# A decoder trunk whose instruction order comes from a table of durations, with rotary scores on 128 rows

## The chip, the core and the metric

The kernel runs on one core of a Trainium2 chip. The metric is the device time of one execution in microseconds, as the median of repeated runs. On the core, TensorE (PE) does matmuls and transposes, VectorE (DVE) and ScalarE (ACT) do elementwise work, GpSimd (POOL) and SyncE (SP) issue DMAs here. PE has a weight load of its own before each matmul (PEld), which overlaps the matmul ahead.

## The reference

Two layers, each: half a SwiGLU step, a mixing block, half a SwiGLU step, on 256 tokens of 1024 features, all in float32:

```python
for l in range(2):
    h = h + 0.5 * swiglu(rms_norm(h, ln_ffn1[l]), ffn1_w13[l], ffn1_w2[l])      # 1024 -> 2 x 2816 -> 1024
    u = rms_norm(h, ln_mix[l])
    z, xbc, dt_raw, cq, ckv, kr, gates = split_cols(u @ w_in[l], IN_SPLIT_SIZES)
    y_ssd = ssd_branch(z, xbc, dt_raw, ...)     # conv of 4 taps, softplus(dt), chunked scan, 32 heads of 64, norm, w_out
    y_mla = mla_branch(cq, ckv, kr, cos, sin, ...)
    g = sigmoid(gates)
    h = h + (g[..., :1024] * y_ssd + g[..., 1024:] * y_mla) @ w_o[l]
    h = h + 0.5 * swiglu(rms_norm(h, ln_ffn2[l]), ffn2_w13[l], ffn2_w2[l])

# in mla_branch, for each of 8 heads: 128 unrotated and 64 rotated features
q = concatenate([q[..., :128], apply_rope(q[..., 128:], cos, sin)], -1)          # after rms_norm over 192
k = concatenate([k[..., :128], apply_rope(k[..., 128:], cos, sin)], -1)          # the rotated part is one for all heads
scores = where(causal, (q @ k.T) * 192 ** -0.5, -inf)                            # in two blocks of 128 queries
out = softmax(scores) @ v
```

## The kernel before

Activations lie transposed, features on the 128 partitions and the 256 tokens along the row. All weights come from HBM in float32 blocks, mostly 128x1024, in the order of use: SP's DMA brings a block to `st`, ACT rounds it to fp32r in `wh` (L152), DVE takes the difference `wl` (L153); four blocks are in flight. An activation operand (X, A, oT) is split the same way into a high and a low half. A product is then three matmuls of 256 columns per 128 features (`mm`, L169 to L171) or one of 512 and one of 256 (`mm2`, L178 and L179).

The stages of a layer are ffn 1, the mix and ffn 2. The mix begins with the projections for the latents of query and key-value, the softplus chain of dt (L501 to L524: a dozen small DVE steps, each of which reads the one before) and the cumulative sums of dA (L527, L528). Then follows a loop whose order `loop_order` writes out: for j in 0..7 the SSD of four heads (`ssd`), one attention head (`head`), and in between the convolution of the next channels, the projections of the next pair of heads, and so on. In the SSD the products of dec and xdt (L658) are 64 wide. A norm is: squares summed into acc, matmuls with ones (L241), a reciprocal root on DVE of nine small steps that each read the one before (`row_factor`, L249 and L216 to L224), and a broadcast by matmul (L256).

`head` works on head h, with i = h % 2 its place in a pair. It transposes the unrotated query and key (L761) and copies them to qkT; for i = 0 it also transposes the rotated query and key of the pair (L770: 64 features of each head, 128 rows together) and copies both to peT (L771). Scores are, for each of two blocks of queries, a product of qkT on 128 rows (L779) and one of peT on the 64 rows of head i (L780), added in PSUM, then a mask by matmul (L781). Softmax takes maxima on DVE (L784), exponentials with sums on ACT (L792), a reciprocal on DVE (L794) and a scaling on ACT; the result is transposed (L799) and multiplied with the values (L803, L804).

The program is written stage after stage. The scheduler of the framework (with its own timeline model, L905) decides the order on each engine, under the dependences of tiles and the numbers of buffers; in each ffn but the first, and in the mix, `issue_after` holds a part back until a named instruction (L388, L390, L437). An instruction waits on its own engine's queue, so what stands behind it waits too.

Of the kernel before, what the change touches and what calls it, by code (L numbers as in the profile page):

```python
# [2 lines left out]

# [1 line left out]

# [13 lines left out]
P = 128  # L19
L = 2  # L20
T = 256
# [14 lines left out]
XSB, ZB = 2, 1  # L36
STBUF = 4
GB, SB, HB = 4, 2, 2


V_LN1, V_LNM, V_LN2 = 0, 8, 16
# [16 lines left out]
NC_ = 672  # L58


class Build:
    def __init__(self, ctx, tc, a, out):
        self.tc, self.nc, self.a, self.out = tc, tc.nc, a, out
        nc = self.nc
        pool = lambda n, b=1, **k: ctx.enter_context(tc.tile_pool(name=n, bufs=b, **k))
# [142 lines left out]
    def rsqrt(self, x, n, tag):  # L208

        nc = self.nc  # L210
        y = self.tmp(tag + "y", [P, n])
        t = self.tmp(tag + "t", [P, n])
        tt, stt = nc.vector.tensor_tensor, nc.vector.scalar_tensor_tensor
        c = 0.703952253
        s = math.sqrt(0.375 * c)
        nc.vector.tensor_scalar(out=y.bitcast(I32), in0=x.bitcast(I32), scalar1=-0.5, scalar2=float(0x5F1FFFF9),  # L216
                                op0=ALU.mult, op1=ALU.add)
        tt(out=t, in0=y, in1=y, op=ALU.mult)
        stt(out=t, in0=t, scalar=-1.0, in1=x, op0=ALU.mult, op1=ALU.mult)
# [4 lines left out]
        self.last = stt(out=y, in0=t, scalar=5.0 * s * s, in1=y, op0=ALU.add, op1=ALU.mult).ins  # L224
        return y

    def square_into(self, acc, src, first):
# [8 lines left out]
    def row_ms(self, acc, scale, tag):  # L236

        nc = self.nc
        ps = self.sps()
        for c in range(2):  # L240
            self.summed = nc.tensor.matmul(ps[:, c:c + 1], lhsT=acc[:, c * P:(c + 1) * P], rhs=self.ones,  # L241
                                           start=True, stop=True).ins
        return ps

    def row_factor(self, acc, n, tag):
# [43 lines left out]
    def tables(self, cb, pos):  # L289
# [11 lines left out]
        for c in range(2):  # L301
            nc.vector.tensor_scalar(out=ang[:, c * 32:(c + 1) * 32], in0=inv, scalar1=posf[:, c:c + 1], scalar2=None,
                                    op0=ALU.mult)
        two_pi = 2.0 * math.pi
        parts, rest = [], two_pi
        for bits in (9, 9, 9):
# [70 lines left out]
    def ffn(self, l, which, X, Xn, gain_next, late=lambda: None):  # L377
# [5 lines left out]
        first = not self.used  # L383
        for i in range(KF):
            gu = self.tmp("t2", [P, 2, T])
            with ExitStack() as order:
# [4 lines left out]
                for g in range(2):  # L391
                    ps = self.gps()
                    m = KD // (2 if self.used < 4 else 1)
                    for k in range(0, KD, m):
                        self.mm2(ps, self.w("w13"), m, X, k, k == 0, k + m == KD)
                    self.halves(gu[:, g, :], ps)
# [21 lines left out]
    def mix(self, l, X0, Xn, gain, gain_next):  # L418
# [15 lines left out]
            self.square_into(acc2[q], ps, i in (0, 4))  # L434


        with self.tc.issue_after(self.last):  # L437
            ps = self.gps()[:, :T]
            self.mm(ps, self.w("dk"), KD, X0, 0, True, True)
            pg = self.gps()  # L440
            for g in range(2):
                self.mm(pg[:, g * T:(g + 1) * T], self.w("gate"), KD, X0, 0, g == 0, g == 1)
            latent(0)
# [59 lines left out]
        e = self.tmp("dte", [P, 2, 32], bufs=1)  # L503
        stt(out=e, in0=x, scalar=-1.0, in1=x, op0=ALU.mult, op1=ALU.max)
        act(out=e, in_=e, func=AF.Exp, scale=-1.0)
        d = self.tmp("dtd", [P, 2, 32], bufs=1)
# [4 lines left out]
        q = self.tmp("dtq", [P, 2, 32], bufs=1)  # L511
# [238 lines left out]
    def head(self, S, h):  # L750
# [11 lines left out]
        act(out=qkT[:, 0, :], in_=pn[:, :T], func=AF.Copy, scale=v[:, V_GQ:V_GQ + 1])  # L762
        act(out=qkT[:, 1, :], in_=pn[:, T:], func=AF.Copy, scale=v[:, V_GK:V_GK + 1])
        if i == 0:
            peT = self.tmp("peT", [P, 2, T], bufs=1)
# [41 lines left out]
    def run(self):  # L807
# [10 lines left out]
        for l in range(L):  # L818
# [91 lines left out]
```

## Time and profile before

| | us |
|---|---|
| median of 3 runs (lowest, highest) | 1468.09 (1467.69, 1468.92) |
| the profiled execution, its time and its span | 1469.72, 1467.8 |
| PE busy | 1451.8 |
| PE weight loads | 1304.8 |
| DVE busy | 1114.6 |
| ACT busy | 911.8 |

Busy time is the sum over the span. An engine's idle time costs something only where the chain of work that ends last goes through it. A matmul's end is modelled, so neighbouring ones overlap in the rows: the cost of one is read from its start to the start of the next. x2 in a timeline row means two equal instructions in succession; a float32 matmul shows as two passes.

### The profile page before, as it was taken

What the parts mean: (1) busy time and instruction counts of PE and PEld (TensorE: products, weight loads), DVE (VectorE), ACT (ScalarE), POOL (GpSimd) and SP (SyncE); (2) the same over time, 40 slices, a digit from 0 to 9 for tenths busy, and PEclk for the clock granted to TensorE, in tenths of its full rate; (3) what the DMA queues carried; (4) which work ended last, traced back from release to release, by engine and by line L of the source; (5) the groups of instructions that cost most, each with busy time, mean ns of one, the idle gap of its engine ahead of it and who ended that gap; (6) DMA issues with size and microseconds to landing.
All of it is one profiled execution on the core that took longest, in us unless ns stands there. A gap on an engine that the chain in (4) does not pass through costs nothing.

```text
span 1467.8 us, 25011 instructions
## 1 busy us (share of the span) xinstructions
PE 1451.8 (99%) x9418; PEld 1304.8 (89%) x9418; DVE 1114.6 (76%) x2080; ACT 911.8 (62%) x1738; POOL 18.5 (1%) x38
## 2 busy tenths in 40 slices
PE   7999999999999999999999999999999999999999
PEld 6888899899888999888888888997998889988888
DVE  7877679888877677777678776888888576688764
ACT  6555556988775456555455554678888654565542
POOL 0000000000000000000000000000000000000000
PEclk9999999999999999999999999999999999999999
DMA  7556655555444555556655566565554445555563
GB/s 254 184 186 178 192 176 182 183 160 157 152 144 158 188 179 188 191 189 183 193 191 191 188 180 195 178 192 155 166 169 139 154 165 190 175 190 193 187 197 109
DMA packets 75977, 261.43 MB, mean 178 GB/s; under 512 B 8880, under 2 KB 11184, under 8 KB 75856
## 3 DMA queue, kind: packets, MB, share of 16 engines
q1 hardware_dynamic: 73232, 251.37, 53.3%
q0 software_dynamic: 2624, 8.46, 1.9%
q8 instruction: 74, 1.21, 0.3%
q14 instruction: 47, 0.39, 0.1%
HBM read 258.68 MB, written 1.11 MB: 177 GB/s over the span
## 4 chain that ended last, share of the span: by engine, by line
PE 97%; DVE 1%; ACT 1%; issue 0%; DMA 0%; SPq 0%; DVEq 0%; ACTq 0%
PE g L178 40%; PE g L179 21%; PE g L169 9%; PE g L170 9%; PE g L171 9%; PE g L695 2%; PE s L658 2%; PE g L719 1%; PE h L780 1%; PE h L779 1%; PE h L761 0%; PE s L635 0%; PE h L803 0%; DVE wl L153 0%; DVE cy L594 0%; PE h L799 0%
## 5 line engine op out<-in xcount | busy, mean ns | idle before, releaser
L152 ACT CAST wh<-st 128x1024 fp32r<-128x1024 f32 (+2 forms) x488 | 500.6, 1027 | 483.5 <-PE g L178 314.7
L153 DVE TENSOR_TENSOR wl<-st,wh 128x1024 fp32r<-128x1024 f32 (+2 forms) x488 | 581.0, 1192 | 258.6 <-ACT wh L152 254.7
L178 PE MATMUL g<-X,wh 128*128 128x512 f32 x928 | 330.8, 399 | 8.0 <-DVE X L205 7.5
L178 PE MATMUL g<-A,wh 128*128 128x512 f32 x938 | 327.6, 395 | 0.0
L179 PE MATMUL g<-X,wl 128*128 128x256 f32 x928 | 262.6, 283 | 0.0
L179 PE MATMUL g<-A,wl 128*128 128x256 f32 x938 | 260.8, 279 | 0.0
L178 PE MATMUL g<-oT,wh 128*128 128x512 f32 x704 | 244.5, 392 | 0.0
L169 PE MATMUL g<-X,wh 128*128 128x256 f32 x768 | 219.6, 287 | 1.2 <-DVE cy L594 1.2
L178 PEld LDWEIGHTS g<-X,wh 128*128 128x128 f32 x928 | 175.8, 189 | 49.3 <-DVE X L205 8.3
L170 PE MATMUL g<-X,wh 128*128 128x256 f32 x768 | 218.7, 285 | 0.0
L171 PE MATMUL g<-X,wl 128*128 128x256 f32 x768 | 218.4, 285 | 0.0
L178 PEld LDWEIGHTS g<-A,wh 128*128 128x128 f32 x938 | 175.7, 188 | 40.1
L179 PE MATMUL g<-oT,wl 128*128 128x256 f32 x704 | 196.9, 280 | 0.0
L179 PEld LDWEIGHTS g<-X,wl 128*128 128x128 f32 x928 | 177.1, 191 | 0.4 <-issue 0.2
L179 PEld LDWEIGHTS g<-A,wl 128*128 128x128 f32 x938 | 176.6, 188 | 0.4
L178 PEld LDWEIGHTS g<-oT,wh 128*128 128x128 f32 x704 | 131.6, 187 | 28.6
L169 PEld LDWEIGHTS g<-X,wh 128*128 128x128 f32 x768 | 146.7, 191 | 3.2 <-issue 1.6
L170 PEld LDWEIGHTS g<-X,wh 128*128 128x128 f32 x768 | 146.9, 191 | 0.7 <-issue 0.5
L171 PEld LDWEIGHTS g<-X,wl 128*128 128x128 f32 x768 | 146.9, 191 | 0.3 <-issue 0.3
L179 PEld LDWEIGHTS g<-oT,wl 128*128 128x128 f32 x704 | 133.0, 189 | 0.2
L170 PE MATMUL g<-oT,wh 128*128 128x256 f32 x272 | 76.8, 283 | 0.0
L171 PE MATMUL g<-oT,wl 128*128 128x256 f32 x272 | 76.6, 284 | 0.0
(286 smaller groups left out, 1831.0 us busy)
## 6 DMA issues: line engine op xcount, KB each, us to landing
st<-in_w_dram SPq DMA_DIRECT2D x238, 512.0 KB, 4.3
st<-in_win_dram SPq DMA_DIRECT2D x124, 512.0 KB, 4.0
st<-in_wso_dram SPq DMA_DIRECT2D x32, 512.0 KB, 4.1
st<-in_w_dram SPq DMA_DIRECT2D x32, 384.0 KB, 3.2
row<-rows POOLq DMA_DIRECT2D x32, 256.0 KB, 3.9
st<-in_wmo_dram SPq DMA_DIRECT2D x16, 512.0 KB, 4.2
st<-in_wo_dram SPq DMA_DIRECT2D x16, 512.0 KB, 3.5
st<-in_wuq_dram SPq DMA_DIRECT2D x16, 384.0 KB, 3.3
```

The lines of the kernel that those rows point to most:

```text
L152: self.nc.scalar.copy(wh, st)
L153: self.nc.vector.tensor_tensor(out=wl, in0=st, in1=wh.bitcast(F32), op=ALU.subtract)
L169: mm(out, lhsT=wh[:, k, :], rhs=xh, start=start and k == 0, stop=False)
L170: mm(out, lhsT=wh[:, k, :], rhs=xl, start=False, stop=False)
L171: mm(out, lhsT=wl[:, k, :], rhs=xh, start=False, stop=stop and k == nk - 1)
L178: mm(out, lhsT=wh[:, k, :], rhs=X[:, x0 + k, :], start=start and k == 0, stop=False)
L179: mm(out[:, :T], lhsT=wl[:, k, :], rhs=X[:, x0 + k, :T], start=False, stop=stop and k == nk - 1)
L658: nc.tensor.matmul(py[64 * i:64 * i + 64, q * T + c * P:(q + 1) * T], lhsT=xdt[:, c, f:f + 64], rhs=r[:, i, o:o + n], start=q == 0 and c = ...
L695: nc.tensor.matmul(pc[c], lhsT=aa, rhs=ww, start=k == 0 and i == 0, stop=k == 3 and i == 2)
L719: nc.tensor.matmul(pc[c], lhsT=aa, rhs=ww[:, k, :], start=k == 0 and i == 0, stop=k == 1 and i == 2)
L779: mm(o, lhsT=qkT[:, 0, cs], rhs=qkT[:, 1, ks], start=c == 0, stop=False)
L780: mm(o, lhsT=peT[:, 0, cs], rhs=peT[:, 1, ks], start=False, stop=False)
```

## The change

Two things change. First, the kernel no longer hands its instructions to the framework as it goes. `Order` records every call with the regions of tiles that it reads and writes. Then `arrange` runs through a schedule of its own: each engine, when free, takes the first of its next 12 ready steps (in program order) whose inputs are there by a table of durations (`cost` for the pitch on the engine, `TAIL` for the latency to another engine); for PE the inputs have to be there 250 ns earlier. The steps are emitted in the order of the times that come out, with the framework's own ordering off. `issue_after` is gone. The softplus's small tiles share the buffer of `kn`.

Second, the rotary product of the scores runs on all 128 rows: the query goes to `qz`, which has one plane for each head of the pair, with zeros in the other head's 64 rows; the key stays whole in `keT`.

```diff
+LOOK, MARGIN = 12, 250.0
...
+    TAIL = {"PE": 190.0, "ACT": 140.0, "DVE": 120.0, "POOL": 200.0, "SP": 0.0}
...
+    def cost(engine, name, args, kw):
...
+        if engine == "PE":
+            if name == "transpose":
+                return 109.0, 0
+            n, dt = size(kw["rhs"]), kw["lhsT"].tile.what[1]
+            if dt == F32R:
+                return n / 2.4 + 13.5, 0
...
+        t = 66.0 + 1.042 * n
+        if name == "scalar_tensor_tensor":
+            t += 60.0
+        return t, 0
...
+    def arrange(self):
...
+            for index, s in sorted(waiting[e], key=lambda x: x[0])[:LOOK]:
+                at = room(s)
+                if at is None:
+                    continue
+                at = max(at, s.ready)
+                margin = MARGIN if e == "PE" else 0.0
+                if at <= now and max(s.far, 0.0) + margin <= now:
+                    pick = s
+                    break
...
+                end = now + s.pitch + s.tail
...
+            for n in s.then:
+                near = n.engine == e and s.tail >= 0
+                n.ready = max(n.ready, now + s.pitch if near else end)
+                if not near:
+                    n.far = max(n.far, end)
...
+    def emit(self):
+        take = lambda v: v.take() if isinstance(v, View) else v
+        for s in self.arrange():
+            s.call(*(take(v) for v in s.args), **{k: take(v) for k, v in s.kw.items()})
...
+        self.qz = cp.tile([P, 2, T], F32, name="qz")
+        nc.vector.memset(self.qz, 0.0)
...
-                if i == 0 and not first:
-                    order.enter_context(self.tc.issue_after(self.last))
-                if i == 1 and not first:
-                    order.enter_context(self.tc.issue_after(self.summed))
...
-        x = self.tmp("dtx", [P, 2, 32], bufs=1)
+        small = self.tmp("kn", [P, 2, 2, P], bufs=1)
+        x, e, d, q = (small[:, :, 0, i * 32:(i + 1) * 32] for i in range(4))
...
-            nc.scalar.copy(peT, pp.rearrange("p (i t) -> p i t", i=2))
-            S["peT"] = peT
-        peT = S["peT"][64 * i:64 * i + 64]
+            for e in range(2):
+                nc.scalar.copy(self.qz[64 * e:64 * e + 64, e, :], pp[64 * e:64 * e + 64, :T])
+            S["keT"] = self.tmp("keT", [P, T], bufs=1)
+            nc.scalar.copy(S["keT"], pp[:, T:])
+        keT = S["keT"]
...
-            mm(o, lhsT=peT[:, 0, cs], rhs=peT[:, 1, ks], start=False, stop=False)
+            mm(o, lhsT=self.qz[:, i, cs], rhs=keT[:, ks], start=False, stop=False)
...
+        with self.tc.manual_schedule():
+            nc.emit()
```

What the new order moves is shown at three places, as the rows of an engine's queue.

**The score block on PE, in a head of the first layer's loop.** Before, the block stands between weight matmuls (g<-X,wh) and SSD products (s<-dec,xdt); qkT holds the unrotated parts of query and key, peT the rotated ones of two heads:

```order
L169 MATMUL g<-X,wh 128x256
L170 MATMUL g<-X,wh 128x256
L779 MATMUL h<-qkT 128x128
L780 MATMUL h<-peT 128x128
L779 MATMUL h<-qkT 128x256
L780 MATMUL h<-peT 128x256
L781 LDWEIGHTS identb
L781 MATMUL h<-negb,identb 128x2x128
L658 MATMUL s<-dec,xdt 64x256 x2
```

In the changed kernel the engine has, at the same head (every instruction carries line 335, the line of the replay; qz is the padded query, keT the key):

```order
L335 MATMUL s<-dec,xdt 64x256 x2
L335 MATMUL s<-dec,xdt 64x128 x2
L335 MATMUL h<-qkT 128x128
L335 MATMUL h<-keT,qz 128x128
L335 MATMUL h<-qkT 128x256
L335 MATMUL h<-keT,qz 128x256
L335 LDWEIGHTS identb
L335 MATMUL h<-negb,identb 128x2x128
L335 MATMUL g<-X,wh 128x256
```

The block keeps its five steps and their shapes; the rotary products read qz and keT, and the SSD products stand ahead of it.

**DVE at the start of the mix.** Before, the softplus (dtq, L514), the root of the latents' sums (lm, then rly) and others are laced through splits (wl) and convolution taps (cy):

```order
L153 TENSOR_TENSOR wl<-st,wh 128x1024
L514 SCALAR_TENSOR_TENSOR dtq<-dtq,dtd 128x64
L357 TENSOR_TENSOR qp<-qp,rob 128x128
L514 SCALAR_TENSOR_TENSOR dtq<-dtq,dtd 128x64 x2
L153 TENSOR_TENSOR wl<-st,wh 128x1024
L514 SCALAR_TENSOR_TENSOR dtq<-dtq,dtd 128x64
L594 SCALAR_TENSOR_TENSOR cy<-g,vec_87,cy 128x255
L478 SCALAR_TENSOR_TENSOR lm<-s,Rt_2411 128x2
L514 SCALAR_TENSOR_TENSOR dtq<-dtq,dtd 128x64
L594 SCALAR_TENSOR_TENSOR cy<-g,vec_87,cy 128x254
L479 TENSOR_SCALAR lm<-lm 128x4
L514 SCALAR_TENSOR_TENSOR dtq<-dtq,dtd 128x64
```

After, the same links (softplus in kn, the root in lm, rly and rlt, its products in Rc, Rf and Rfac) stand in one string of 32 rows between two splits, of which these are the last part:

```order
L335 SCALAR_TENSOR_TENSOR rly<-rlt,rly 128x4
L335 TENSOR_TENSOR Rc<-rly,rhy 128x2 x2
L335 TENSOR_TENSOR Rf_2520<-Rc 128x4
L335 TENSOR_SCALAR Rf_2520<-Rf_2520 128x4
L335 TENSOR_SCALAR Rfac<-Rc 128x2
L335 COPY Rfac<-Rc 128x2
L335 SCALAR_TENSOR_TENSOR kn<-kn 128x2x32 x6
L335 TENSOR_SCALAR kn<-kn 128x2x32
L335 SCALAR_TENSOR_TENSOR dt<-kn 128x64
L335 SCALAR_TENSOR_TENSOR dA<-dt,expA 128x64
L335 TENSOR_SCALAR dth<-dt 128x64
L335 TENSOR_TENSOR wl<-st,wh 128x1024
```

Links that had other work between them now follow each other directly; the string ends in dA, dth and the next split.

**PE at the same place.** Before, the matmuls with dA (L527, L528) stand among weight matmuls, with a transpose of the rotary query:

```order
L169 MATMUL g<-X,wh 128x256
L170 MATMUL g<-X,wh 128x256
L171 MATMUL g<-X,wl 128x256
L770 MATMUL h<-cb,qp 128x128
L527 MATMUL s<-dA,cb 128x32 x2
L528 MATMUL s<-dA,cb 128x32
L770 MATMUL h<-cb,qp 128x128
```

After, the second sum matmul (s<-ones,accs) is followed by four matmuls of 384 columns and these twelve of 512, two transposes, the matmuls with dA, and directly the transposes of acum, the copy that DVE makes of their result:

```order
L335 MATMUL g<-wh,A 128x512
L335 MATMUL g<-wl,A 128x512
L335 MATMUL g<-wh,A 128x512 x2
L335 MATMUL g<-wl,A 128x512
L335 MATMUL g<-wh,A 128x512 x2
L335 MATMUL g<-wl,A 128x512
L335 MATMUL g<-wh,A 128x512 x2
L335 MATMUL g<-wl,A 128x512
L335 MATMUL g<-wh,A 128x512
L335 MATMUL h<-cb,qn 128x128 x2
L335 MATMUL s<-dA,cb 128x32 x3
L335 MATMUL s<-cb,acum 32x128 x2
```

What DVE has to do from the sums to dA now lies beside this stretch of PE alone.

**PE from a sum matmul to the broadcast, at the end of the mix.** Before (seventeen weight matmuls lie between s<-ones,acc and s<-cb,rhy; these are the last five):

```order
L178 MATMUL g<-oT,wh 128x512
L179 MATMUL g<-oT,wl 128x256
L178 MATMUL g<-oT,wh 128x512
L179 MATMUL g<-oT,wl 128x256
L178 MATMUL g<-oT,wh 128x512
L256 MATMUL s<-cb,rhy 128x128 x2
```

After, the whole stretch:

```order
L335 MATMUL s<-ones,acc 128x1 x2
L335 MATMUL g<-oT,wh 128x512
L335 MATMUL g<-oT,wl 128x256
L335 MATMUL g<-oT,wh 128x512
L335 MATMUL g<-oT,wl 128x256
L335 MATMUL g<-oT,wh 128x512
L335 MATMUL g<-oT,wl 128x256
L335 MATMUL g<-oT,wh 128x512
L335 MATMUL g<-oT,wl 128x256
L335 MATMUL g<-oT,wh 128x512
L335 MATMUL s<-cb,rhy 128x128 x2
```

The broadcast moved up, to the tenth row behind the sums.

## Rows read from the trace of the kernel before

**Rows 1.** The page: span, busy time by engine, chain that ended last

```profile
span 1467.8 us, 25011 instructions
...
PE 1451.8 (99%) x9418; PEld 1304.8 (89%) x9418; DVE 1114.6 (76%) x2080; ACT 911.8 (62%) x1738; POOL 18.5 (1%) x38
...
PE 97%; DVE 1%; ACT 1%; issue 0%; DMA 0%; SPq 0%; DVEq 0%; ACTq 0%
```

**Rows 2.** Stretches: PE, PEld, DVE, ACT, POOL busy (instructions), PEclk, DMA share, GB/s

```profile
0.00:16.00 16.00, 8.50 (x25) 6.77 (x26) 10.16 (x31) 11.45 (x25) 0.20 (x4) 1.00 0.82 271
...
280.00:285.50 5.50, 3.53 (x23) 2.57 (x21) 5.50 (x11) 5.50 (x18) 0.54 (x1) 1.00 0.56 178
285.50:289.00 3.50, 3.27 (x9) 2.72 (x10) 3.31 (x10) 3.50 (x12) 0.54 (x1) 0.51 0.63 202
289.00:400.00 111.00, 111.00 (x852) 102.21 (x850) 94.43 (x207) 90.84 (x209) 4.29 (x8) 1.00 0.50 157
...
1005.00:1014.00 9.00, 6.86 (x41) 5.09 (x40) 8.06 (x20) 9.00 (x27) 1.07 (x2) 1.00 0.60 179
...
1460.00:1467.80 7.80, 4.29 (x36) 4.09 (x35) 0.42 (x1) 0.00 (x0) 0.00 (x0) 0.92 0.05 17
```

**Rows 3.** Timeline of PE, a score block: start, us, engine, line, out<-in, tile, shape

```profile
298.31 0.38 PE L779 MATMUL h<-qkT 128*128 128x128 f32 x2
298.62 0.49 PE L780 MATMUL h<-peT 64*128 64x128 f32 x2
299.04 0.70 PE L779 MATMUL h<-qkT 128*128 128x256 f32 x2
299.67 0.70 PE L780 MATMUL h<-peT 64*128 64x256 f32 x2
300.30 0.28 PE L781 MATMUL h<-negb,identb 128*128 128x256 bf16 x1
```

**Rows 4.** Timeline of PE, value products and transposes just before that block

```profile
293.92 0.59 PE L803 MATMUL h<-pT,vv 128*128 128x256 f32 x2
294.35 0.38 PE L804 MATMUL h<-pT,vv 128*128 128x128 f32 x2
294.56 0.38 PE L761 MATMUL h<-cb,qn 128*128 128x128 f32 x2
294.78 0.38 PE L761 MATMUL h<-cb,kn 128*128 128x128 f32 x2
```

**Rows 5.** Timeline of PE around the first stall of the loop

```profile
282.25 0.39 PE L719 MATMUL g<-wl,A 128*128 128x512 f32 x1
282.48 0.40 PE L719 MATMUL g<-wh,A 128*128 128x512 f32 x1
...
285.73 0.76 PE L719 MATMUL g<-wh,A 128*128 128x512 f32 x1 [2.19 <-DVE sm L794]
...
288.42 0.41 PE L169 MATMUL g<-X,wh 128*128 128x256 f32 x1
```

**Rows 6.** Timeline of DVE, links of the softplus

```profile
235.99 0.22 DVE L514 SCALAR_TENSOR_TENSOR dtq<-dtq,dtd 128x64 f32<-128x64 f32 x1
236.12 0.28 DVE L357 TENSOR_TENSOR qp<-qp,rob 128x128 f32<-128x128 f32 x1
236.32 0.48 DVE L514 SCALAR_TENSOR_TENSOR dtq<-dtq,dtd 128x64 f32<-128x64 f32 x2
```

**Rows 7.** Timeline of DVE, the reciprocal root: first, last, and what follows

```profile
204.46 0.16 DVE L249 TENSOR_SCALAR rhm<-s 128x2 f32<-128x2 f32 x1 [3.27 <-PE s L241]
...
206.04 0.16 DVE L224 SCALAR_TENSOR_TENSOR rhy<-rht,rhy 128x2 f32<-128x2 f32 x1
206.11 1.22 DVE L153 TENSOR_TENSOR wl<-st,wh 128x1024 fp32r<-128x1024 f32 x1
```

**Rows 8.** Timeline of PE, the sum matmuls and what follows

```profile
203.92 0.51 PE L241 MATMUL s<-ones,acc 128*128 128x1 f32 x4
204.29 0.36 PE L171 MATMUL g<-oT,wl 128*128 128x256 f32 x1
```

More of the change, by code (lines that the diff above doesn't have):

```diff
@@ L1 @@
+import heapq
 import math
 from contextlib import ExitStack
+import einops
 import numpy as np
@@ L58, with __init__, shape, _next @@
 NC_ = 672
+class View:
+    def __init__(self, tile, steps, arr, region, dims):
+        self.tile, self.steps, self.arr, self.region, self.dims = tile, steps, arr, region, dims
+    @property
+    def shape(self):
+        return self.arr.shape
+    def _next(self, step, arr, region=None, dims=None):
+        return View(self.tile, self.steps + (step,), arr, region or self.region, dims)
+    def __getitem__(self, key):
+        key = key if isinstance(key, tuple) else (key,)
+        region, dims = self.region, None
+        if self.dims is not None:
+            p0, p1, lo, _ = region
+            k = key[0]
+            assert isinstance(k, slice)
+            p0, p1 = p0 + (k.start or 0), p0 + (p1 - p0 if k.stop is None else k.stop)
+            dims, hi = [], 0
+            for i, (size, stride) in enumerate(self.dims):
+                k = key[i + 1] if i + 1 < len(key) else slice(None)
+                if isinstance(k, slice):
+                    b, e, _ = k.indices(size)
+                    lo += b * stride
+                    hi += (e - b - 1) * stride
+                    dims.append((e - b, stride))
+                else:
+                    lo += k * stride
+            region = region if self.tile.ring.bank else (p0, p1, lo, lo + hi + 1)
+        return self._next(lambda ap: ap[key], self.arr[key], region, dims)
+    def rearrange(self, pattern, **k):
+        return self._next(lambda ap: ap.rearrange(pattern, **k), einops.rearrange(self.arr, pattern, **k))
+    def unsqueeze(self, d):
+        return self._next(lambda ap: ap.unsqueeze(d), np.expand_dims(self.arr, d))
+    def to_broadcast(self, shape):
+        return self._next(lambda ap: ap.to_broadcast(shape), np.broadcast_to(self.arr, shape))
+    def bitcast(self, dt):
+        return self._next(lambda ap: ap.bitcast(dt), self.arr, None, self.dims)
+    def take(self):
+        ap = self.tile.place()
+        for step in self.steps:
+            ap = step(ap)
+        return ap
@@ new lines, with __init__, place @@
+class Later(View):
+    def __init__(self, ring, shape, dt, name):
+        arr = np.broadcast_to(np.zeros((), np.int8), shape)
+        dims, stride = [], 1
+        for n in reversed(shape[1:]):
+            dims.insert(0, (n, stride))
+            stride *= n
+        super().__init__(self, (), arr, (0, shape[0], 0, stride), dims)
+        self.ring, self.what, self.name = ring, (shape, dt), name
+        self.real, self.writes, self.reads, self.left, self.free_at = None, [], [], 0, 0.0
+        self.placed = False
+        self.number = len(ring.tiles)
+        ring.tiles.append(self)
+    def place(self):
+        if self.real is None:
+            self.real = self.ring.pool.tile(*self.what, name=self.name, tag=self.ring.tag, bufs=self.ring.bufs)
+        return self.real
@@ new lines, with __init__, tile @@
+class Ring:
+    def __init__(self, pool, tag, bufs, bank):
+        self.pool, self.tag, self.bufs, self.bank, self.tiles, self.next = pool, tag, bufs, bank, [], 0
+class Pool:
+    def __init__(self, real, bufs, bank):
+        self.real, self.bufs, self.bank, self.rings = real, bufs, bank, {}
+    def tile(self, shape, dt, name=None, tag=None, bufs=None):
+        tag = tag or name
+        ring = self.rings.setdefault(tag, Ring(self.real, tag, bufs or self.bufs, self.bank))
+        return Later(ring, list(shape), dt, name)
@@ L61 @@
 class Build:
     def __init__(self, ctx, tc, a, out):
-        self.tc, self.nc, self.a, self.out = tc, tc.nc, a, out
-        nc = self.nc
-        pool = lambda n, b=1, **k: ctx.enter_context(tc.tile_pool(name=n, bufs=b, **k))
+        self.tc, self.a, self.out = tc, a, out
+        nc = self.nc = Order(tc.nc)
+        pool = lambda n, b=1, **k: Pool(ctx.enter_context(tc.tile_pool(name=n, bufs=b, **k)), b, n.startswith("ps"))
         self.cp = pool("cp")
@@ L223, in rsqrt @@
         stt(out=t, in0=t, scalar=-10.0 / 3.0 * s, in1=t, op0=ALU.add, op1=ALU.mult)
-        self.last = stt(out=y, in0=t, scalar=5.0 * s * s, in1=y, op0=ALU.add, op1=ALU.mult).ins
+        stt(out=y, in0=t, scalar=5.0 * s * s, in1=y, op0=ALU.add, op1=ALU.mult)
         return y
@@ L240, in row_ms @@
         for c in range(2):
-            self.summed = nc.tensor.matmul(ps[:, c:c + 1], lhsT=acc[:, c * P:(c + 1) * P], rhs=self.ones,
-                                           start=True, stop=True).ins
+            nc.tensor.matmul(ps[:, c:c + 1], lhsT=acc[:, c * P:(c + 1) * P], rhs=self.ones,
+                                           start=True, stop=True)
         return ps
@@ L382, in ffn @@
         A = self.new_A()
-        first = not self.used
         for i in range(KF):
             gu = self.tmp("t2", [P, 2, T])
-            with ExitStack() as order:
-                if i == 0 and not first:
-                    order.enter_context(self.tc.issue_after(self.last))
-                if i == 1 and not first:
-                    order.enter_context(self.tc.issue_after(self.summed))
[L391 to L396, printed above, removed]
+            for g in range(2):
+                ps = self.gps()
+                m = KD // (2 if self.used < 4 else 1)
+                for k in range(0, KD, m):
+                    self.mm2(ps, self.w("w13"), m, X, k, k == 0, k + m == KD)
+                self.halves(gu[:, g, :], ps)
             nc.vector.tensor_tensor(out=gu, in0=gu, in1=Rb2, op=ALU.mult)
@@ L434, in latent @@
             self.square_into(acc2[q], ps, i in (0, 4))
[L437 to L443, printed above, removed]
+        ps = self.gps()[:, :T]
+        self.mm(ps, self.w("dk"), KD, X0, 0, True, True)
+        pg = self.gps()
+        for g in range(2):
+            self.mm(pg[:, g * T:(g + 1) * T], self.w("gate"), KD, X0, 0, g == 0, g == 1)
+        latent(0)
         Rb = self.bcast(Rt, None)
@@ L498, in mix @@
         self.rope(kpr, tm[:, :, :64], self.ropes[1])
-        x = self.tmp("dtx", [P, 2, 32], bufs=1)
+        small = self.tmp("kn", [P, 2, 2, P], bufs=1)
+        x, e, d, q = (small[:, :, 0, i * 32:(i + 1) * 32] for i in range(4))
         tt(out=x, in0=tm[:, :, 64:96], in1=v[:, V_DTB:V_DTB + 32].unsqueeze(1).to_broadcast([P, 2, 32]), op=ALU.add)
-        e = self.tmp("dte", [P, 2, 32], bufs=1)
         stt(out=e, in0=x, scalar=-1.0, in1=x, op0=ALU.mult, op1=ALU.max)
         act(out=e, in_=e, func=AF.Exp, scale=-1.0)
-        d = self.tmp("dtd", [P, 2, 32], bufs=1)
         ts(out=d, in0=e, scalar1=2.0, scalar2=None, op0=ALU.add)
@@ L510, in mix @@
         tt(out=d, in0=e, in1=e, op=ALU.mult)
-        q = self.tmp("dtq", [P, 2, 32], bufs=1)
         ts(out=q, in0=d, scalar1=1.0 / 15.0, scalar2=None, op0=ALU.mult)
@@ L764, in head @@
         if i == 0:
-            peT = self.tmp("peT", [P, 2, T], bufs=1)
             pp = self.hps()
```

133 lines of the change are left out of this document (added).

## The prediction

> **What bounds the kernel now.** I read the page first: TensorE is busy for 1451.8 of 1467.8 us and the chain that ended last is 97% PE [rows 1]. So time can come from two places only: the 16.0 us in which PE stood, and matmuls that hold PE longer than their work needs. DVE has 1114.6 us and ACT 911.8 us of work, so both have slack over the whole span, but that is an average over stages.
>
> The table of stretches says where PE stood [rows 2]. 7.5 us go before 16 us (the first weights come in) and 3.5 us after 1460 us (the last result goes out). 2.0 us lie in 280 to 285.5 and 2.1 us in 1005 to 1014, both in the mix loop; the remaining 0.9 us is scattered. The same table shows the mix loop of the first layer (289 to 400): PE 111.00 of 111.00 us, DVE 94.43. That is the stage in which DVE has least to spare.
>
> The other place is in the score block. The timeline of PE [rows 3] has it from 298.31 to 300.30: 0.31 for the qkT pair of 128 columns, 0.42 for the peT pair of 128, 0.63 for the qkT pair of 256, 0.63 for the peT pair of 256, together 1.99 us. (A pair is the two passes of one f32 matmul.) A few us earlier stand pairs of the same sizes among their own kind [rows 4]: 0.43 us from the start of L803 (256 columns) to the next line, 0.21 from L804 (128) to the next. At those prices the block is 2 x (0.21 + 0.43) = 1.28 us. What differs is the tile: peT is 64\*128, the rows around it 128\*128, and each of the four pairs follows a pair of the other kind. So two round trips between the kinds cost 0.71 us, 0.35 each. That the price sits on the change of kind and not on the 64 rows is read from the qkT pairs: they are 128\*128 and dear too (0.31 and 0.63).
>
> **Step 1, the rotary scores on 128 rows.** The products keep their columns and get the prices of [rows 4]; their other 64 rows are multiplied by the zeros in qz. 16 heads x 0.71 = **-11.4 us**. Bounds: 0 if the dear pairs are due to something else (see C), -11.4. I take the far end, as the pairs of [rows 4] are the same sizes on 128 rows. What it adds is one clearing of qz at the start, while PE still waits for weights, and per pair of heads two more small copies on ACT, which has 20 of 111 us free in the loop [rows 2]: nothing.
>
> The Trainium skill's page "TensorEngine Tiling (Array Packing)", section "Theoretical Speedup", speaks against this step: a contraction of at most 64 rows may be up to twice as fast as a 64-row tile. By it the padded pairs would cost up to the 1.05 us of the two peT pairs once more per block, +16.8 us. The trace disagrees here: the 64-row pair of 128 columns takes 0.42, the 128-row one of [rows 4] 0.21, and nothing runs beside it.
>
> **Step 2, fewer changes of tile elsewhere.** The SSD products with dec are 128\*64 tiles. Counted in the two orders, they stand in 21 separate groups before and in 16 after. No row isolates their change of kind; the bounds are 0 and 5 x 0.35. I take 0.3 each, since the round trip above is the nearest: **-1.5 us**.
>
> **Step 3, the old waits.** The two stalls in the loop belong to the old order: at 285.73 PE was released by DVE's reciprocal of a softmax sum, ahead of a key-value matmul [rows 5]. Both places are gone in the new order, in which 3.7 to 5 us of PE work (counted in its rows, at the prices used here) lie between the scores and what needs their softmax: -2.0 and -2.1. After the first stall the granted clock read 0.51 in 285.5 to 289 [rows 2], the lower of the two levels (1.2 GHz), and six matmuls of 512 took 285.73 to 288.42, 2.69 us, in place of 6 x 0.23 (282.25 to 282.48) = 1.38: another -1.3. After the second the clock stayed at 1.00. Sum **-5.4 us**. The ends: 0 to -5.4.
>
> **Step 4, the new waits.** The table's weakness is one sentence of its code: a step that follows another on the same engine is ready at its pitch, with no latency. The trace has that latency. On DVE, L514 at 235.99 is followed by an unrelated step after 0.13 us, but of the two L514 at 236.32, of which the second reads the first, the second ends 0.48 after, so starts 0.26 after it [rows 6]. The chain of the reciprocal root says the same: 1.58 us from 204.46 to 206.04 over eight steps, 0.2 each, while the unrelated split after its last step starts 0.07 later [rows 7]. So a dependent pair costs about 0.125 us more than the table says. Counted in the orders, DVE has 163 such neighbours before and 503 after: 340 x 0.125 = 43 us of DVE time, some 100 pairs (12.5 us) of it in each layer's mix loop. The old order put big splits between the links; the new one strings the links together. What PE sees of it:
>
> (a) Mix start, once per layer. Between the second sum matmul and the matmul with dA, PE has 4 matmuls of 384 columns (0.17 each, from 0.23 for 512), 12 of 512 and two transposes (0.11, from 294.56 to 294.78 [rows 4] for two): 0.7 + 2.8 + 0.2, and 0.1 of the sums, 3.8 us. DVE, from that sum to dA, has ten links of a rsqrt at 0.2, six steps on its result at 0.16 (the duration of one [rows 7]), eight links of softplus at 0.26 [rows 6] and one single 0.13: 5.2 us, and 0.6 for the sum matmul and the two hand-overs. PE waits 5.8 - 3.8 = 2.0 us. Then the transposes of acum stand directly behind; acum waits for the copy on DVE, in front of which a split of 1.2 us [rows 7] is queued: 0.3 to 1.5, I take 1.1, as the split is likely to be under way. Together 3.1, twice: **+6.2 us** (bounds 0, if PE has more cover than I count, and 7).
>
> (b) From a sum matmul to the broadcast that needs its root, at five places. The chain takes 203.92 to 204.46 and on to 206.20, 2.28 us [rows 7, 8], and a hand-over of 0.05. The old order had 17 matmuls there, the new one nine: five of 512 and four of 256 (0.12, half of the 0.23 for 512), 1.6 us, and 0.4 for the sums themselves [rows 8]. PE waits 2.33 - 2.0: 5 x 0.35 = **+1.8 us**, between 0 and 4.
>
> (c) The loop. Of the 12.5 us per layer some 9 fall into 289 to 400, so DVE goes from 94.4 to about 103 of 111 us: still not the bound, but with less to catch up in. The taps of the convolution, once spread, now stand three in a row. Nothing to 12.5 us per layer; nearer to nothing, since a wait once taken leaves every later link that much slack. I take 2: **+4 us**.
>
> **Sum.** -11.4 - 1.5 - 5.4 + 6.2 + 1.8 + 4 = -6.3 us. The profiled execution took 1469.72 us (its span and 1.9 around it); that gives 1463.4. It is 1.6 above the median of the three runs, 1468.09, so against that median **1461.8 us**.
>
> **Rivals.**
> A. *The new waits do not come.* If dependent steps cost DVE no more than others, or PE has more cover at these places than I count, step 4 is 0: 1461.8 - 12.0 = 1449.8 us. For it: PE has some work at each place, and its margin of 250 ns. Against it: the 0.26 and 0.13 of [rows 6]. The Trainium skill has a rule for this case: its page "VectorE: DVE Perf Modes", section "The DRAIN you can't avoid", says that the next op does not start until the pipe is empty, and that a chain with a semaphore after each op takes as long as one without. By it a dependent step would cost no more than another, and the table would be right. The two rows disagree.
> B. *DVE becomes the bound of the loop.* If the strings fall where DVE is already late, all 12.5 us per layer show on PE: +21 more than my 4 (twice 12.5 less 4), 1482.8 us, slower. It decides once step 4 exceeds the 18.3 us of steps 1 to 3, that is with (c) above 10.3 us. For it: DVE's 103 of 111 us. Against it: PE's own delay gives the slack back. With half of it (12.5 us in place of my 4) the time is 1470.3.
> C. *Padding does nothing.* If the dear pairs are dear because a product's two factors come from other tiles (new weights from another buffer), not because of the kind of tile, step 1 is 0: 1473.2 us. For it: L779's pairs are dear as well. Against it: in [rows 4] the buffers change from pair to pair too, at 0.21.
>
> **How the numbers follow.** The forecast gets 0.51, A (all or most of it) 0.26, half of B 0.11, B 0.07, C 0.05. Two runs of this kernel differ by up to 0.1%, so 0.2%, 2.9 us, is about what can be told from no change. Faster: the forecast and A, 0.77. Within 0.2%: half of B, 0.11. Slower: B and C, 0.12. The range goes from A with a little more of step 2 (1448) to half of B (1471). The likeliest case alone spans 1457 to 1466, from the bounds of (a) and (b).
>
> **What would show it.** Step 1: the score block at about 1.3 us, and no 64\*128 forms among the matmuls. Step 3: PE idle in the loop below 1 us in each layer apart from (c), no stretch with a low clock. Step 4: PE idle before the matmul with dA and before the transposes of acum, 2.0 and 1.1, and about 0.35 before each broadcast of rhy; DVE's mean for the small links up. I am wrong if those places show no idle time (A), if the loop's PE idle exceeds 15 us with a DVE tile as releaser (B), or if the score block still takes 2 us (C).

## The result, and the profile after

The changed kernel took 1476.14 us in the median of five runs, the kernel before 1468.09: a ratio of 1.0055 (95% interval 1.0043 to 1.0066), slower by half a per cent. One of the five runs, with a mean clock of 0.85, is left out of the ratio. The forecast was 1461.8 and its range ended at 1471.

The page of the profiled execution, the same lines as [rows 1]:

```profile
span 1474.4 us, 25056 instructions
...
PE 1449.2 (98%) x9418; PEld 1309.6 (89%) x9418; DVE 1148.3 (78%) x2081; ACT 928.4 (63%) x1754; POOL 18.6 (1%) x38
...
PE 81%; DVE 11%; ACT 5%; issue 2%; DMA 0%; SPq 0%; DVEq 0%; ACTq 0%
```

PE's idle time rose from 16.0 to 25.2 us, and the chain that ended last now runs through DVE and ACT for 16% of the span. PE's busy time hardly fell, by 2.6 us, though the score blocks alone should have taken 11.4 from it. The stretches, to be read beside [rows 2], say where both come from:

```profile
16.00:24.00 8.00, 7.25 (x27) 6.31 (x27) 5.99 (x16) 3.32 (x5) 0.00 (x0) 0.57 0.64 215
...
236.00:241.00 5.00, 2.16 (x14) 1.39 (x12) 4.52 (x23) 2.41 (x11) 0.00 (x0) 1.00 0.01 2
241.00:246.00 5.00, 4.94 (x29) 4.97 (x30) 4.62 (x20) 3.55 (x10) 0.99 (x2) 0.66 0.63 206
...
289.00:400.00 111.00, 109.53 (x842) 103.05 (x841) 100.22 (x211) 95.44 (x223) 4.30 (x8) 1.00 0.50 159
...
1005.00:1014.00 9.00, 8.99 (x62) 8.40 (x60) 6.72 (x13) 8.87 (x20) 0.76 (x2) 1.00 0.42 134
```

The old stall of 1005 to 1014 is gone (8.99 of 9.00 busy, 6.86 before). The start of the mix lost 2.8 of 5 us, and the clock read 0.66 behind it. The clock also read 0.57 from 16 to 24, a stretch that the forecast did not look at. The loop has 1.47 us of idle PE in 289 to 400 where it had none, with DVE at 100.2 us.

The releasers of PE's waits:

```profile
PE g L335 <- DVE X L335: 7.0, 2, 6.7
PE s L335 <- DVE xdt L335: 4.4, 6, 1.2
PE s L335 <- DVE dth L335: 3.9, 2, 2.1
PE g L335 <- ACT wh L335: 1.8, 2, 1.0
PE h L335 <- ACT qkT L335: 1.2, 2, 0.9
PE s L335 <- DVE acum L335: 1.1, 2, 0.7
PE s L335 <- DVE BC L335: 0.8, 1, 0.8
PE g L335 <- DVE rob L335: 0.3, 2, 0.2
```

The first line is the program's start, as before. dth (made right behind dA, in the string) and acum are the mix start in both layers; xdt, qkT and BC are the loops; wh is at 15 us.

A score block, on PE, beside [rows 3]:

```profile
323.37 0.49 PE L335 MATMUL h<-qkT 128*128 128x128 f32 x2
323.69 0.39 PE L335 MATMUL h<-keT,qz 128*128 128x128 f32 x2
323.92 0.60 PE L335 MATMUL h<-qkT 128*128 128x256 f32 x2
324.35 0.59 PE L335 MATMUL h<-keT,qz 128*128 128x256 f32 x2
324.78 0.27 PE L335 MATMUL h<-negb,identb 128*128 128x256 bf16 x1
```

It takes 1.41 us in place of 1.98, and 1.31 where it does not follow the 64-column SSD products. (These are blocks with no other work between their steps; 8 of the 16 have some.)

The mix start, DVE and then PE:

```profile
236.75 1.51 DVE L335 SCALAR_TENSOR_TENSOR kn<-kn 128x64 f32<-128x64 f32 x6
...
238.66 0.23 DVE L335 SCALAR_TENSOR_TENSOR dA<-dt,expA 128x64 f32<-128x64 f32 x1
...
239.09 1.23 DVE L335 TENSOR_TENSOR wl<-st,wh 128x1024 fp32r<-128x1024 f32 x1
240.24 0.22 DVE L335 COPY acum<-s 128x64 f32<-128x64 f32 x1
```

```profile
236.56 0.38 PE L335 MATMUL h<-cb,qn 128*128 128x128 f32 x2
239.03 0.83 PE L335 MATMUL s<-dA,cb 128*128 128x32 f32 x6 [2.09 <-DVE dth L335]
240.51 0.40 PE L335 MATMUL s<-cb,acum 128*32 128x128 f32 x2 [0.65 <-DVE acum L335]
```

Six links of 64 columns take 1.51 us, 0.26 each as in [rows 6]; PE stands until dA is there, then again for the copy behind a split. And one place of the loop, PE and DVE at 400 us:

```profile
400.16 0.36 PE L335 MATMUL g<-X,wh 128*128 128x256 f32 x1
401.69 1.52 PE L335 MATMUL s<-dec,xdt 128*64 128x256 f32 x16 [1.17 <-DVE xdt L335]
```

```profile
398.33 0.42 DVE L335 TENSOR_TENSOR kp<-kpr,rqy 128x256 f32<-128x256 f32 x1
398.66 2.35 DVE L335 TENSOR_TENSOR wl<-st,wh 128x1024 fp32r<-128x1024 f32 x2
...
401.21 0.42 DVE L335 TENSOR_TENSOR xdt<-s,dth 128x256 f32<-128x256 f32 x1
```

xdt stands behind two splits, and these behind a string of a reciprocal root (rqt, rqy, kp) at 0.2 us a link.

### The profile page after: what moved, and what is told of

Its sections match the earlier page's. It is cut to its first block, busy times and chain, and to the rows that moved or that the text cites. A ratio compares the mean times of both kernels' runs of the same rounds, so it can differ in the third digit from the quotient of the medians.

```text
span 1474.4 us, 25056 instructions
## 1 busy us (share of the span) xinstructions
PE 1449.2 (98%) x9418; PEld 1309.6 (89%) x9418; DVE 1148.3 (78%) x2081; ACT 928.4 (63%) x1754; POOL 18.6 (1%) x38
## 4 chain that ended last, share of the span: by engine, by line
PE 81%; DVE 11%; ACT 5%; issue 2%; DMA 0%; SPq 0%; DVEq 0%; ACTq 0%
PE g L335 77%; DVE wl L335 4%; PE h L335 2%; PE s L335 2%; ACT dec L335 2%; DVE cy L335 2%; DVE dec L335 1%; ACT wh L335 1%; ACT pp L335 1%; DVE kn L335 0%; ACT A L335 0%; ACT cy L335 0%; DVE rqt L335 0%; DMA st<-in_w_dram 0%; DVE qp L335 0%
## 5 line engine op out<-in xcount | busy, mean ns | idle before, releaser
L335 PE MATMUL g<-X,wh 128*128 128x256 f32 (+1 forms) x2464 | 617.7, 329 | 9.1 <-DVE X L335 7.0
L335 PE MATMUL g<-oT,wh 128*128 128x512 f32 (+1 forms) x1248 | 343.8, 344 | 0.0
L335 PE MATMUL g<-A,wh 128*128 128x512 f32 (+1 forms) x982 | 336.9, 389 | 0.0
L335 PEld LDWEIGHTS g<-oT,wh 128*128 128x128 f32 x1248 | 216.1, 189 | 29.6
L335 PEld LDWEIGHTS g<-oT,wl 128*128 128x128 f32 x976 | 184.9, 189 | 0.0
L335 DVE TENSOR_TENSOR t<-t,g 128x256 f32<-128x256 f32 x180 | 74.7, 415 | 0.5 <-ACT t L335 0.5
L335 DVE SCALAR_TENSOR_TENSOR cy<-g,vec,cy 128x255 f32<-128x255 f32 x144 | 68.9, 480 | 6.8 <-ACT cy L335 2.7
L335 ACT COPY t<-g 128x256 f32<-128x256 f32 x180 | 65.1, 362 | 0.3 <-PE g L335 0.3
L335 DVE TENSOR_TENSOR t<-t,Rb 128x512 f32<-128x512 f32 x88 | 60.9, 692 | 3.0
L335 PE MATMUL g<-wh,A 128*128 128x384 f32 (+1 forms) x192 | 55.4, 357 | 0.0
```

Of the source, the lines that this page charges most:

```text
L335: s.call(*(take(v) for v in s.args), **{k: take(v) for k, v in s.kw.items()})
```

## The experiments

The theory after the result: the order is right by its own table, but the table leaves out the latency between dependent steps on one engine, so DVE, and perhaps ACT, are later than PE's queue expects. Rivals: any more cautious table would do as well; the order is bad for another reason (look-ahead, changes of tile); the 128 rows gain nothing.

**The two parts apart.** The first kernel has the rotary edit of the change and the softplus tiles in kn's buffer, under the old scheduler; the second is the changed kernel with the old lines of `head`:

```diff
-            mm(o, lhsT=self.qz[:, i, cs], rhs=keT[:, ks], start=False, stop=False)
+            mm(o, lhsT=peT[:, 0, cs], rhs=peT[:, 1, ks], start=False, stop=False)
```

> The kernel before, in its old order, with the rotary products on 128 rows (and the softplus tiles in the buffer of kn, which makes the room for it). If the changes of tile cost what was read (in the changed kernel the score block fell from 1.98 to 1.31 to 1.42 us, 16 times), this alone gives 1468.1 - 10 = 1458 us, and the order costs the rest of the difference to 1476. If padding gives nothing, 1468.

Measured 1471.26 us, ratio 1.0030 (1.0017 to 1.0043): slower, against the expected 1458. The blocks with nothing between their steps took 1.31 us (0.67 less, as priced; one, in a stretch whose clock read 0.67, took 1.98), but the old scheduler, given other steps, made another order, with waits that the kernel before does not have:

```profile
PE h L804 <- ACT pT L802: 4.9, 3, 2.2
PE g L169 <- ACT ta L727: 2.6, 1, 2.6
```

So one edit under a scheduler is not one edit of the order, and this run says nothing of the sum.

> The changed kernel with the rotary products back on 64 rows: the recorded order alone. If both parts add up: 1476.1 + 10 = 1486 us, the order alone 18 us slower than the old one. If the block gains nothing from 128 rows: 1476.

1480.95 us, ratio 1.0092 (1.0078 to 1.0106). The order alone loses 13 us; the 128 rows gain 4.8 in it by the whole time, half of what the blocks say. (Where the other half is, the table of the rotary's other half shows.)

**The latency in the table.**

```diff
+NEAR = {"DVE": 125.0}
...
-                n.ready = max(n.ready, now + s.pitch if near else end)
+                n.ready = max(n.ready, now + s.pitch + NEAR.get(e, 0.0) if near else end)
```

> The changed kernel with one number more in its table: a DVE step that needs the one before on DVE is ready 125 ns later. If the missing latency makes the new waits, the mix start (3.2 and 2.7 us of PE waiting), the low clock after it (1.6) and most of the 8.8 us of waits in the two loops go: 1463 us, 1466 if the loop keeps half. If the waits come from the order's look-ahead or from ACT, 1473 to 1476.

1459.57 us, ratio 0.9947 (0.9935 to 0.9960): 16.6 us faster than the changed kernel, and faster than the kernel before. The first lines of its list of PE's waits:

```profile
PE g L336 <- DVE X L336: 7.3, 2, 6.7
PE g L336 <- DVE wl L336: 0.7, 1, 0.7
PE g L336 <- DVE kn L336: 0.7, 2, 0.4
PE s L336 <- DVE accs L336: 0.6, 2, 0.3
```

dth and xdt are no longer among them, and the clock was 1.0 in all five runs (0.996 to 0.998 in the changed kernel's). The time of the mixes is read from the sum matmul at the end of the ffn ahead (s<-ones,acc) to the one at the end of the mix; in the changed kernel these start at 205.18, 563.62, 932.22 and 1289.54 us. Both mixes together fell from 715.8 to 703.8 us, by 12.0; the rest of the gain lies in the ffns, which differ by some 3 us each between traces for another reason (last section). So single comparisons below are given for the mixes too, from one trace of each kernel. DVE at the mix start now alternates two strings, so that each link's latency lies beside a link of the other:

```profile
233.77 0.23 DVE L336 SCALAR_TENSOR_TENSOR kn<-kn 128x64 f32<-128x64 f32 x1
233.91 0.15 DVE L336 SCALAR_TENSOR_TENSOR rly<-rlt,rly 128x4 f32<-128x4 f32 x1
234.03 0.23 DVE L336 SCALAR_TENSOR_TENSOR kn<-kn 128x64 f32<-128x64 f32 x1
```

**Controls: more caution without the links.** First `MARGIN` 1000 for 250, then `66.0` to `96.0` in DVE's pitch:

> The changed kernel with a margin of 1000 ns for PE in place of 250, the table else unchanged. If the waits are lateness of any kind that slack heals, the loops' 8.8 us of waits go and the mix start is halved: 1465 us. If the wider margin makes the table itself leave PE without ready work, or the missing latency adds up beyond 1 us everywhere, 1474 or more.

> A control to the run with the latency: every DVE step is 30 ns longer in the table, dependent or not, which adds the same DVE time in sum (2081 x 30 = 62 us; 503 dependent neighbours x 125 = 63). If what matters is that the latency sits on the links of a string, this heals a third of it at most: the 32 small steps of the mix start get 1 of 3.2 us; about 1471 us. If any more cautious table for DVE would do, 1460 as with the latency.

1467.43 us (ratio 1.0001, 0.9992 to 1.0010) and 1470.11 us (1.0021, 1.0009 to 1.0033). Both heal about half or less; in the mixes 2.6 and 5.1 us of the 12.0. The second leaves the string where it was and only eases the loop:

```profile
PE s L335 <- DVE dth L335: 5.2, 2, 2.6
PE s L335 <- DVE xdt L335: 1.4, 6, 0.4
```

**Which links.** The same latency for a part of DVE's steps: all with a pitch below 205 ns; of these only the mix start's (kn, lm, rly, rlt, Rc, Rf, Rfac, dt, dA, dth, rlm); of these all but the mix start's.

```diff
-now + s.pitch + NEAR.get(e, 0.0) if near else end
+now + s.pitch + (NEAR.get(e, 0.0) if s.pitch < 205.0 and s.tiles[0].name in START else 0.0) if near else end
```

> The latency of 125 ns only behind DVE steps of up to 130 columns (softplus, reciprocal roots, softmax's small ones), not behind convolution taps and other wide steps. If mix start and loop are two separate costs, the mix start goes (3.2 + 2.7, and the low clock of 1.6) and the loops' 8.8 us of waits on xdt and others stay: 1468.5 us. If the loop's waits come from the small steps as well, 1460.

> The latency behind the small DVE steps of the mix start alone (softplus, the root of the latents, their products). If the mix start is worth what its waits say (5.9 us, and 1.7 for the low clock after it), 1468.5 us, and the loops' waits on xdt stay. If a right start sets the loop right too, 1460 or less.

> The latency behind all other small DVE steps (the roots of the norms and of each head pair, softmax). If the loops' waits come from these, 8.8 us go and the mix start stays: 1467 us. If they come from the mix start's lateness, carried on, 1475.

1457.15 (ratio 0.9930, 0.9919 to 0.9942), 1466.46 (0.9997, 0.9986 to 1.0008) and 1461.26 us (0.9956, 0.9943 to 0.9968). Against the changed kernel: 19.0, 9.7 and 14.9 us faster, and in the mixes 11.2, 7.6 and 8.5. The 7.6 of the mix start is what its waits and low clock were said to be worth (5.9 and 1.7). The waits of the two partial runs nearly complement each other; with the mix start priced:

```profile
PE s L337 <- DVE xdt L337: 4.7, 6, 1.2
PE s L337 <- DVE BC L337: 1.3, 2, 0.6
```

and with the others priced:

```profile
PE g L337 <- DVE rob L337: 1.8, 2, 0.9
PE s L337 <- DVE dth L337: 1.7, 2, 0.9
```

So the loops' waits come from small links too (roots and softmax), not from the wide taps that the forecast named, and are worth about as much as the mix start. The two parts do not add up (7.6 and 8.5 against 11.2 together).

**The rotary's other half.** ACT gets 130 ns, with DVE's latency or alone, each on 128 and on 64 rows.

> The table with the DVE latency, but the rotary products on 64 rows. If the score block's 0.6 us shows in full once the waits are gone: 1459.6 + 9.5 = 1469 us. If it is worth only the 5 us by which the changed kernel beat its order alone: 1464.5.

> The latency of 125 ns on DVE and 130 ns on ACT (in the trace an ACT step that needs the one before starts 0.13 us later than one that does not). If ACT's links hold up PE in what is left of waits with the DVE latency (some 4 us in the mixes), 1457 us; ACT has more slack than DVE, so if they do not matter, 1459 to 1460.

> The table with latencies on DVE and ACT, and the rotary products on 64 rows. The score block is 0.6 us shorter on 128 rows in every trace so far, 9.5 us in all, but the whole gained only 4.4 to 4.8 in two pairs of runs. If ACT (which makes 16 copies more for the 128 rows) took the rest, the full 9.5 should show now that its links are priced: 1463.5 us. If the rest is lost in another way, 1458.5.

> The changed kernel with the latency of 130 ns on ACT alone. It gave 5.6 us on top of DVE's. If the two add up: 1470.5 us, with the waits on dA at the mix start unchanged (3.9 us). If ACT's links matter only once DVE's are priced: 1475.

> The same with the rotary products on 64 rows. If ACT's missing latency is what takes half of the gain of the 128 rows, this is 9.5 us slower than the run before: 1480 us if that is 1470.5. If the half is lost because PE runs into DVE's waits earlier, the difference stays near 5: 1475.5.

| latency in the table | 64 rows, us | 128 rows, us | gain, us |
|---|---|---|---|
| none | 1480.95 | 1476.14 | 4.8 |
| DVE | 1463.99 | 1459.57 | 4.4 |
| ACT | 1480.93 | 1470.26 | 10.7 |
| DVE and ACT | 1464.34 | 1453.94 | 10.4 |

The ratios to the kernel before are 0.9977 (0.9967 to 0.9988), 0.9908 (0.9895 to 0.9920), 0.9974 (0.9963 to 0.9986), 1.0023 (1.0004 to 1.0042) and 1.0085 (1.0069 to 1.0101), in the order of the expectations. The run with ACT alone spread from 1466.8 to 1480.8, so its 10.7 is the weakest number of the table.

By these times the blocks' full price shows only where ACT's links are priced. The traces say that this is mostly not so. The same table for the two mixes, where all the blocks lie:

| latency in the table | 64 rows, mixes, us | 128 rows, mixes, us | gain, us |
|---|---|---|---|
| none | 724.2 | 715.8 | 8.4 |
| DVE | 710.1 | 703.8 | 6.4 |
| ACT | 721.9 | 711.8 | 10.1 |
| DVE and ACT | 708.6 | 699.5 | 9.1 |

In the mixes the 128 rows gain most of the blocks' 9.5 us in every pair. What halves the gain of the first two pairs lies in the first ffn: its sum comes 5.4 and 3.9 us later in the trace with 128 rows, and 2.7 and 3.5 us earlier in the other two pairs. Of the rotary edit only the clearing of qz on DVE lies there, and it does not make the sum late: the runs with ACT's latency alone and with the mix start's alone have it too, and their sums are early (199.15 and 199.11; last section). ACT's latency is worth 2.3 and 1.5 us in the mixes on 64 rows, and 4.0 and 4.3 on 128, the form that has 16 more copies on ACT: some 2 to 3 us of the gain may hang on it, not half. DVE's latency is worth 12.0 to 14.0 us there in all four pairs.

**Three more tables.** On both latencies: a margin of 500; 150 ns for each change of PE between 128- and 64-column tiles; DVE's latency only behind small steps.

```diff
+                narrow = s.kw.get("out", s.args[0] if s.args else None).arr.shape[0] == 64
+                s.pitch += 150.0 * (narrow != self.narrow)
```

> Latencies on DVE and ACT and a margin of 500 ns for PE. PE still waits some 2.6 us in the mixes. If these are late by less than half a microsecond, 1452 us; if the margin only pushes work about, 1454 or more.

> Latencies on DVE and ACT, and 150 ns more on PE in the table for each change between 128-column and 64-column tiles (16 to 19 groups, a round trip costs about 0.3 us in the traces). The order is then right by about 5 us over the program, which changes when the table thinks other engines are due. If such drift of the table is what leaves the small waits: 1452 us. If PE being later than the table only gives the others slack, no change: 1454.

> The latency behind small DVE steps (up to 130 columns) and on ACT. The small steps alone did better than all of DVE by 2.4 us (1457.2 against 1459.6). If that is more than the luck of one order, it holds with ACT: 1451.5 us; if it is such luck, 1453 to 1457.

1461.19 (0.9958, 0.9947 to 0.9970), 1462.10 (0.9959, 0.9945 to 0.9973) and 1453.18 us (0.9903, 0.9890 to 0.9915). The last is the fastest kernel of the study, 1% below the kernel before and 23 us below the changed one; on 1457.15 it repeats that ACT's latency gives some 4 us. The margin's loss is not in the mixes, which took 1.8 us less than without it (697.7 against 699.5): see the last section. Why a truer price for tiles lost 8 us was not found. Its trace is 12.5 us longer than that with both latencies: 5.4 up to the sum of the first ffn (some 3 of it the effect of the last section) and 7.2 in the mixes, with waits of 1.2 us each for keT and qkT (1.6 and 0.2 without the price); it may be no more than one order's bad luck, and then single comparisons of a few microseconds prove little here. What the study rests on are the 12 to 14 us that the latency on DVE gives in the mixes (16 to 17 of the whole time) in four pairs, and the 6 to 10 us of the 128 rows in the same four.

## Why the prediction was wrong

The forecast was -6.3 us and the span grew by 6.6. The step that failed is 4 (c), the loops: forecast at +4, measured at +8.5. Three smaller errors go the same way: step 1 gave 9.5 us and not 11.4, and two terms stood at nothing, the low clock behind the first mix start (1.7) and the first 30 us (2.6). By the starts of PE's matmuls, compared with what each shape takes at its steady rate, the forecast's terms came out like this:

| term | forecast, us | measured, us |
|---|---|---|
| score blocks (measured 16 x (1.98 - 1.39)) | -11.4 | -9.5 |
| fewer groups of 64-column tiles (measured 5 x 0.28) | -1.5 | -1.4 |
| old stalls and their low clock | -5.4 | -5.4 |
| (a) mix start, both layers | +6.2 | +6.4 |
| (b) sum to broadcast (measured 5 x 0.37) | +1.8 | +1.8 |
| (c) loops | +4 | +8.5 |
| low clock behind the first mix start | 0 | +1.7 |
| first 30 us | 0 | +2.6 |

These make +4.7 of the +6.6 us by which the span grew; the rest was not taken apart, but some 0.9 us of it is a slower rate late in the first ffn (last section). In the list of waits (c) is the 6.4 us of xdt, qkT and BC. The list shows less than the table: a matmul's end is modelled late, so a part of a late start is shown as busy (0.16 of the 0.26 us in the rows below).

- **Steps 2, 3, (a) and (b)** held, place by place. At the end of the first mix the broadcast starts 0.49 us after the 512-column matmul before it, where 0.23 is its rate, and takes 0.46 itself, 0.11 more than unhindered:

```profile
565.45 0.39 PE L335 MATMUL g<-oT,wh 128*128 128x512 f32 x1
565.94 0.71 PE L335 MATMUL s<-cb,rhy 128*128 128x128 f32 x4
566.40 0.36 PE L335 MATMUL g<-oT,wl 128*128 128x256 f32 x1
```

  Four other places read the same. For (a) the wait before dA was forecast at 2.0 us and its idle time reads 2.09. The latency of a DVE link is the cause, shown by the runs that price it: with the mix start's links alone priced, the mixes fall by 7.6 us.
- **Step (c) failed by size.** I took 2 us a layer because a wait, once taken, gives slack back; 4.3 were lost. The runs with half of the links priced show that the small steps of roots and softmax made most of it, not the taps (with these alone priced the mixes fall by 8.5 us and xdt leaves the list, though dth's wait at the mix start shrinks too, from 3.9 to 1.7). DVE did not become the bound (100.2 of 111 us), so rival B (1482.8 us) is not what happened, though (c) came out between my 4 and the 12.5 of its half: PE waited for late single steps while DVE had 10% to spare.
- **Step 1 was right in its mechanism and too large in size.** A block fell by 0.57 to 0.67 us and not by 0.71, as most stand right behind SSD products of 64 columns and take 1.41. (One reading was loose: the first pair of the block does not follow another kind of tile. Its start-to-start time holds the change behind it.) "20 of 111 us free" on ACT was read as "the copies cost nothing". In the mixes the 128 rows gained 8.4 us with nothing priced, 1.1 less than the blocks, and ACT's latency gave 1.7 to 2.8 us more on 128 rows than on 64, so the copies did cost something; that they are the cause is not shown apart from that.
- **Not in the sum at all:** the change moved the first 24 us too. Two waits for wh there, of 1.04 and 0.75 us, were followed by a stretch at clock 0.57. I looked for low clock only behind the old stalls, and not behind the new waits that I forecast. Whether this term belongs to the change is open: the run with ACT's latency alone has the same order on PE, DVE and ACT in its first 195 us and a clock of 1.00 there, and the run with DVE's latency behind the small steps has the same two waits (1.00 and 0.75 us) and a clock of 1.00 behind them:

```profile
16.00:24.00 8.00, 7.00 (x41) 5.91 (x42) 7.46 (x17) 5.71 (x8) 0.00 (x0) 1.00 0.69 214
```

```profile
16.00:24.00 8.00, 7.25 (x43) 6.22 (x43) 7.80 (x21) 5.14 (x7) 0.00 (x0) 1.00 0.77 268
```

- **Rival A** would have been the time if dependent steps cost no more. The Trainium skill, page "VectorE: DVE Perf Modes", section "The DRAIN you can't avoid", says that the next op does not start until the pipe is empty, lets an op that is not held start earlier, and says that a semaphore after each op costs nothing extra. Here an independent DVE step starts some 82 to 84 ns before the profile's end of the one ahead, and a dependent one 34 ns after it (medians; 558 dependent neighbours in the changed kernel), and pricing just that turned the order from 0.55% slower to 0.53% faster.
- **Rival C** is out: 1.31 us for the block on 128 rows under either scheduler, where nothing stands between its steps and the clock is full.

## What to carry to other kernels

A list scheduler driven by a table is as good as the table's worst omission: pitches close to the trace (a split of 1024 columns: 1133 ns in the table, 1142 in the trace) were not enough, since it packed dependent steps next to each other exactly where the table said that this is free. Put the latency between dependent steps on the same engine in, for each engine, before tuning margins; here a margin or a general padding healed only part (2.6 and 5.1 of 12.0 us in the mixes). And read an order for strings: the longest run of links between two things that the bounding engine waits for, times the latency, is a first estimate of what it can cost. At the mix start the prediction counted 24 links, 3.0 us, and 3.2 were measured in each layer; an engine at 90% of a stretch did not hide it. And before a gain is put down to one edit, take the trace apart by stages: here a stage with the same order of instructions moved by 6 us, and hid half of a gain.

## What the runs showed that was not expected

The pairs of one 512- and one 256-column matmul that fill an ffn run at one of two steady rates, mostly for a whole stage, with PE fully busy and the clock at 1.00 in both. Rows of the stretches, the run with both latencies first and the one with a margin of 500 second:

```profile
600.00:700.00 100.00, 100.00 (x578) 88.17 (x578) 76.58 (x118) 56.69 (x97) 0.00 (x0) 1.00 0.60 188
```

```profile
600.00:700.00 100.00, 100.00 (x568) 86.76 (x567) 75.18 (x115) 55.17 (x96) 0.00 (x0) 1.00 0.59 184
```

578 matmuls in 100 us against 568: a pair takes 346.7 or 353.3 ns. The difference is about 3.3 us for an ffn. The run with the margin had three of its four ffns at the slower rate, some 10 us, which is more than its loss against the run without. In the changed kernel the first ffn was at the slower rate from end to end, in the kernel before up to about 150 us: some 0.9 us of the result. In the table of pairs one ffn was at the slower rate in the traces of none, DVE and ACT on 128 rows and of both on 64, and none in the other four, so this alone shifts those gains by 3 us, down three times and up once.

The rate does not follow from the order of the instructions. The changed kernel and the run with ACT's latency alone have the same order on PE, DVE and ACT in the first 195 us, and the sum at the end of that ffn stands 6.0 us apart: 3.0 from the first 42 us, with the low clock, and 3.0 from the rate. The changed kernel first:

```profile
205.18 0.50 PE L335 MATMUL s<-ones,acc 128*128 128x1 f32 x4
```

```profile
199.15 0.50 PE L336 MATMUL s<-ones,acc 128*128 128x1 f32 x4
```

So 6 us of the changed kernel's traced time do not follow from the order of that stage (the kernel before has its own stretch at the slower rate); whether they come anew with each execution or stay with a kernel is open, as each has one trace. It may be why runs of one kernel differ by several microseconds; what sets the rate was not tried.

ACT has the same latency as DVE: a dependent step starts 32 ns after the profile's end of the one ahead (69 neighbours), an independent one some 95 ns before it.
